# Up to six SwiGLU pairs instead of seven kept for the output stage, with a fourth piece buffer, loads ahead of stores and three late gates moved back

## The chip, the cores and the metric

The kernel runs on one NeuronCore of a Trainium2 chip. TensorE (PE) multiplies, VectorE (DVE), ScalarE (ACT) and GpSimd (POOL) do the elementwise work, and transfers are issued from SyncE's queue (SP) and from POOL. The metric is the device time of one execution in microseconds, lower being better. The changed kernel is compared with the kernel before by the medians of such times.

## The reference

One decoder block for 512 tokens, all in float32. Two token mixers (a gated convolution and a gated linear recurrence) run beside each other and are merged; then comes a SwiGLU channel mixer with 2816 inner channels, and a last normalisation. The change lies in the second half:

```python
    m = jax.nn.sigmoid(z_ga) * y_a + jax.nn.sigmoid(z_gb) * y_b
    x = x + m @ w_mix_out[l]
    h = rmsnorm(x, norm2_g[l])
    x = x + (jax.nn.silu(h @ ffn_w1[l]) * (h @ ffn_w3[l])) @ ffn_w2[l]
return rmsnorm(x, norm_f_g)
```

## The kernel before

Every float32 product is made of three products of rounded halves (high by high, high by low, low by high), which is why most tiles come as an `h` and an `l`. A weight chunk is loaded into a `raw` buffer, ACT casts it to the high half (L123), and DVE or POOL subtracts it to get the low half (L119). The function `weights` keeps four chunks ahead of the one that PE needs.

The stages follow each other on PE: the input projection (tile `z`), the two mixers' outputs (`yb`, `ya`), their mix (`mxr`), the SwiGLU products (`fr`, and `f1`/`f3` for the first pair) and the output product (`or`).

**SwiGLU.** The 22 tiles of 128 inner channels are worked on as 11 pairs, k = 0 to 10. All but the first are computed by Strassen's scheme in Winograd's form, with seven products of quarter blocks in place of eight: class `Seven`. `half()` makes the first product into the PSUM bank r1 and the second into r2; `copy()` (L1461) then has ACT copy r1 to a tile `c11`, because r1 is written again later. `first()` adds r2 to it on DVE, and `out_of` (L1442) turns the sum into one quarter of the result: SiLU on ACT (L1443), then a multiplication on DVE (L1444). `rest()` makes the other products: r3, r1 again (copied to `q` by ACT at L1489), r5, r7, and r1 a third time, and ends three more quarters, the last of them from a tile `c21`. A pair's results are two tiles, `ou{k}` and `ov{k}`. Its turn takes some 21 us.

**Output product.** It is done by the same scheme. Each pair of `ou` and `ov` is first made into operands by `Sevenfold.pair`: a split of `ou` into halves (`ous{k}h` by ACT, `ous{k}l` by DVE), a sum `os` that is split too (`os1p`), and three differences (`oe` twice, `ov` once). `o7.release(keep)` does so for the pairs that wait until only `keep` are left. In `rest()` it is called in the middle of each pair with `KEPT`, a table by k; what is left over is released in the output stage, one pair for each step. After its eleven steps the operands `oe` and `ov` are split in turn (`oeb`, `ovb`).

**Sums of weights.** The scheme needs sums and differences of weight quarters, which are computed on the chip. For `ffn_w1` and `ffn_w3` pieces (`fws`) are loaded during the earlier stages by the generator `make_f_sums`, summed on POOL and stored to DRAM (`fs`). For `ffn_w2`, 21 pieces (`fwso`, 512 KB) and two last ones of `fws` are loaded by POOL's queue during SwiGLU, summed on DVE and stored to DRAM (`ot`, `fs`). Function `out_step` moves these along, twice for each pair. A piece lives in a buffer of the pool `wsums`, of which there are `PIECES`; at the start of the kernel the same buffers hold the input x.

Tiles of 128x512 float32 come from a pool `long` of `SLOTS` buffers and a pool `short` of 5. The order of the work in the SwiGLU and output stages is made by a scheduler from the order in which the code is written, the buffers that are free and `tc.issue_after`, which sets an instruction behind another; each engine then runs its own list in order.

Of the kernel before, what the change touches and what calls it, by code (L numbers as in the profile page):

```python
# [8 lines left out]
F32 = mybir.dt.float32  # L9
# [4 lines left out]
P = 128  # L14
T = 512
# [10 lines left out]
NT = T // P  # L26
# [2 lines left out]
NF = DF // P  # L29


SLOTS, SHORT = 63, 5
RAW = 4
HL = 5
AHEAD = 4
SUMS_BEHIND = 3
# [8 lines left out]

PIECES = 3


OUT_PIECES = {0: "1", 1: "111", 2: "01", 3: "11", 4: "111", 5: "101", 6: "111", 7: "111", 8: "101", 9: "101", 10: "100"}
SEVEN = (1, 2, 3, 4, 5, 6, 7, 8, 9, 10)


BEGUN, BEGUN_LATER = (1, 2), (3,)
# [5 lines left out]
F_LATE, F_AT, OUT_MIX, MIX_LATE_LAG, LATE_LAG = 2, 6, 1, 2, 8  # L61
OUT_IN = 0

KEPT = {2: 1, 3: 2, 4: 3, 5: 4, 6: 5, 7: 6, 8: 7, 9: 7, 10: 7}


ROWS = [
# [18 lines left out]
def tile_block(ctx, tc, a, out):  # L86
# [4 lines left out]
    hls = pool("hls", HL)  # L91
    wsums = pool("wsums", PIECES)
    psum = pool("psum", 6, space=bass.MemoryType.PSUM)
    psum2 = pool("psum2", 2, space=bass.MemoryType.PSUM)

    def tiles(tag, bufs):
        p_ = pool(tag, bufs)
        return lambda name, dtype=F32: p_.tile([P, T], dtype, tag=tag, name=name)

    longt, shortt = tiles("long", SLOTS), tiles("short", SHORT)  # L100
# [5 lines left out]
    def bank(name):  # L106
        return psum.tile([P, T], F32, tag="mm", name=name)

    def bank2(name):
        return psum2.tile([P, T], F32, tag="cv", name=name)  # L110

    vec, act, pe, pool_e = nc.vector, nc.scalar, nc.tensor, nc.gpsimd


    newest = {}
# [5 lines left out]
    def split_to(h, l, full, eng, copy=act.copy):  # L121

        copy(h, full)  # L123
        if eng is None:
            put_off.append((l, full, h.bitcast(F32)))
            return h, l
        last = sub(eng, l, full, h.bitcast(F32))
        newest["sub" if eng is pool_e else "low"] = last.ins
        return h, l
# [16 lines left out]
    def split(name, full, eng, p_=None, copy=act.copy):  # L146
        p_ = p_ or pairt(name)
        return split_to(*p_, full, eng, copy)
# [243 lines left out]
    def piece_load(name, halves, queue=nc.sync):  # L392
        raw = wsums.tile([P, 1024], F32, tag="wsum", name=f"fws{name}")
        n = 1024 // len(halves)
        for h, src in enumerate(halves):
            queue.dma_start(raw[:, h * n : h * n + n].rearrange("p (e n) -> p e n", n=256), src)
        return raw
# [12 lines left out]
    def piece_store(raw, dest, queue=nc.sync):  # L410
        if len(dest.shape) == 4:
            dest = dest.rearrange("p m k n -> p (m k) n")
        return queue.dma_start(dest, raw.rearrange("p (m n) -> p m n", n=256))  # L413

    def make_f_sums():
# [8 lines left out]
        while todo or sums_due or stores_due:  # L424
# [3 lines left out]
            if sums_due and n >= sums_due[0][0]:  # L428
                sums_due.pop(0)[1]()
            if todo and n >= next_at and len(sums_due) + len(stores_due) + (n < stored[0] + STORED_LAG) < PIECES:  # L430
                next_at += SUMS_STEP - (n >= SUMS_DENSE) - (SUMS_EACH[0] <= n < SUMS_EACH[1])
# [80 lines left out]
        queue.dma_start(rowt[b][r : r + m, :P], src)  # L512

    x_nat = a["x"].rearrange("b (t p) d -> p (b t) d", p=P)
    wide = [wsums.tile([P, 1024], F32, tag="wsum", name=f"x{t}") for t in range(PIECES)]
    xt = [[w[:, :T], w[:, T:]] for w in wide] + [[longt(f"x{t}{h}") for h in range(2)] for t in range(PIECES, NT)]

    def load_x(t):
        if t < PIECES:
            nc.sync.dma_start(wide[t], x_nat[:, t, :])  # L520
            return
        for h in range(2):
            nc.sync.dma_start(xt[t][h], x_nat[:, t, h * T : (h + 1) * T])
# [5 lines left out]
    first = [i for i, (lo, _, _) in enumerate(parts) if lo < n_first]  # L529
# [14 lines left out]

    load_x(0)
    load_x(1)

    def rows_turned(c0, c1):
# [15 lines left out]
    def mm3(ps, ws, xs, lo_last=False):  # L564


        n = 3 * len(ws)
        i = 0
        three = [((wh, xh), (wh, xl), (wl, xh)) for (wh, wl), (xh, xl) in zip(ws, xs)]
        if lo_last:  # L570
            three = [q[:2] for q in three] + [q[2:] for q in three]
        for l, r in (q for qs in three for q in qs):
            pe.matmul(ps, l, r, start=i == 0, stop=i == n - 1)  # L573
            i += 1

    def w_tiles(key, kt, ahead=AHEAD):
        h, l = weights(key, ahead)
        return [(h[:, k, :], l[:, k, :]) for k in range(kt)]
# [86 lines left out]
    def first_sums(t):  # L665
        return root(t, half_sum(t))
# [40 lines left out]
    with tc.manual_schedule(engines={ET.PE, ET.Activation, ET.DVE, ET.SP, ET.Pool}):  # L707
# [4 lines left out]
        r1 = first_sums(1)  # L712
# [432 lines left out]
    LO, HI = HALVES  # L1145
# [213 lines left out]
    out_stores, out_n, sums_due = [], [0], []  # L1359
    out_at, out_steps = [None, None], {k: list(v) for k, v in OUT_PIECES.items()}  # L1360

    def due_sums(now=False):
        for entry in list(sums_due):
            entry[0] -= 1
            if now or entry[0] <= 0:
                sums_due.remove(entry)
                with tc.issue_after(newest["now"]), tc.issue_after(newest["low"]):
                    piece_sums(*entry[1], vec)

    def out_step(k):  # L1370
        due_sums(True)
        if out_at[1]:
            with tc.issue_after(newest["full"]):
                out_stores.append(piece_store(*out_at[1], pool_e).ins)
        if out_at[0]:
            sums_due.append([SUMS_BEHIND, out_at[0]])
        out_at[1], out_at[0] = out_at[0], None
        steps = out_steps.get(k)
        if steps and int(steps.pop(0)):
            name, halves, dest = out_todo.pop(0)  # L1380


            with tc.issue_after(([newest["full"]] * 2 + out_stores)[out_n[0]]):
                out_at[0] = piece_load(name, halves, pool_e), dest
            out_n[0] += 1

    def ffn_out(j, p1, p3):
        s_ = shortt(f"si{j}")
        act.activation(s_, p1, AF.Silu)

        def make(cs, dst):
            newest["now"] = vec.tensor_tensor(out=dst, in0=s_[:, cs], in1=p3[:, cs], op=ALU.mult).ins

        o7.tile(j, make)
# [22 lines left out]
    def f_product(k, got, ps, x_, w_, again=False, ahead=AHEAD, between=None):  # L1417
# [3 lines left out]
        for i in range(2):  # L1421
# [17 lines left out]
                emit_to(emitted[0] + 1)  # L1439
            due_sums()  # L1440

    def out_of(c, dst):  # L1442
        act.activation(c[:, LO], c[:, LO], AF.Silu)  # L1443
        newest["now"] = vec.tensor_tensor(out=dst, in0=c[:, LO], in1=c[:, HI], op=ALU.mult).ins  # L1444

    class Seven:
# [13 lines left out]

        def copy(self):  # L1461
            self.c11 = shortt(f"c11_{self.k}")
            act.copy(self.c11, self.r1)

        def first(self):
            add(self.c11, self.r2, self.c11)
            out_of(self.c11, self.uv[0][:, LO])

        def fourth(self, c):

# [12 lines left out]
        def rest(self):  # L1483
            k, got, r1, (u_, v_) = self.k, self.got, self.r1, self.uv
            r3, r5, r7 = bank(f"fr3_{k}"), bank2(f"fr5_{k}"), bank(f"fr7_{k}")
            f_product(k, got, r3, "s4", "b22")
            f_product(k, got, r1, "s2", "t2", True)
            q = shortt(f"q_{k}")
            act.copy(q, r1)  # L1489
            f_product(k, got, r5, "s1", "t1")  # L1490
            add(q, r5, q)
            c12 = shortt(f"c12_{k}")
            add(c12, r3, q)
            out_of(c12, u_[:, HI])
            out_step(k)

            o7.release(KEPT.get(k, 0))
            f_product(k, got, r7, "s3", "t3")
            c21 = self.c21
            if c21 is None:  # L1500
                c21 = shortt(f"c21_{k}")
                act.copy(c21, r7)
            else:
                add(c21, r1, c21)
                add(c21, r7, c21)
            add(q, r7, q)
            out_of(q, v_[:, HI])
            if self.c21 is None:
                f_product(k, got, r1, "a22", "t4", True)
                add(c21, r1, c21)  # L1510
            out_of(c21, v_[:, LO])
            out_step(k)
            o7.uv.append((u_, v_))
            o7.waiting.append((k, u_, v_))
# [36 lines left out]
    for k in range(KF):  # L1551
        if k in SEVEN:
            b = begun.pop(k, None)
            if not b:
                b = Seven(k)
                b.half()
                b.first()
                out_step(k)
            b.rest()
            continue  # L1560
        o7.release(KEPT.get(k, 0))
        o7.kept = KEPT.get(k, 0)
        for j in (2 * k, 2 * k + 1):
            p1, p3 = bank(f"f1_{j}"), bank(f"f3_{j}")
            mm3(p1, w_tiles(f"f1_{j}", ND), h2)
            mm3(p3, w_tiles(f"f3_{j}", ND), h2)
            ffn_out(j, p1, p3)
        out_step(k)
        if k + 1 in SEVEN:
            for j in BEGUN_LATER:  # L1570
                b = begun[j] = Seven(j)
                b.half()
                b.first()
                out_step(k + 1)
                for c in range(4):
                    b.fourth(c)
                b.fourth_end()
# [128 lines left out]
```

## Time and profile before

| | us |
|---|---|
| median of 3 runs | 790.12 |
| lowest and highest of them | 788.48, 792.69 |
| profiled execution, its own time | 787.58 |
| span of its instructions | 785.8 |
| PE busy | 778.2 (99%) |
| DVE busy | 679.3 (86%) |
| ACT busy | 473.5 (60%) |
| POOL busy | 362.9 (46%) |

The span reaches from the first instruction of the program to the last; the rest of the execution's own time lies around it. In the rows of a timeline the first number is the start in microseconds from the start of the span, the second the time taken, and what stands in brackets is the idle time of the engine just before, with what ended it. A busy PE may hold pauses, since the ends of matmuls are modelled; so the starts of successive matmuls are looked at too. "PEld" is the loading of weights into PE.

### The profile page before, as it was taken

Reading aid. Unit: us, or ns where it says so; the run is one execution under the profiler, and the core shown is the slowest. Engines: PE = TensorE matmul, PEld = TensorE weight load, DVE = VectorE, ACT = ScalarE, POOL = GpSimd, SP = SyncE. Lnnn points to the kernel's source line nnn. Section 1 sums busy time; section 2 is a strip of 40 time slices with the busy share of each in tenths; the row PEclk is TensorE's granted clock in tenths of the full one; section 3 lists DMA queues with packets and bytes.
Section 4 is the critical chain, followed back from the end, with each engine's and each line's share of the span. In section 5 each row is a group of like instructions: output and inputs, shape, how many; then the busy total and the mean of one; then the engine's idle time right before and its main releaser. Section 6 shows DMA issues by size and latency. Waiting matters only on the chain.

```text
span 785.8 us, 12508 instructions
## 1 busy us (share of the span) xinstructions
PE 778.2 (99%) x4328; PEld 680.6 (87%) x4328; DVE 679.3 (86%) x1074; ACT 473.5 (60%) x696; POOL 362.9 (46%) x353
## 2 busy tenths in 40 slices
PE   9999999999999999999999999999999999999996
PEld 8988888888888888888888898999999999888885
DVE  6389998889987987999799869897887889999956
ACT  7543678966785786574245676445445555556844
POOL 4367876789788989754530380122323322000000
PEclk9999999999999999999999999999999999999999
DMA  7657989899999868998978575699999999878652
GB/s 225 189 144 211 267 225 269 230 277 272 260 266 280 266 195 251 309 299 285 314 252 297 172 216 181 193 306 307 308 335 331 314 315 318 268 235 278 194 172 108
DMA packets 188561, 199.04 MB, mean 253 GB/s; under 512 B 15290, under 2 KB 149586, under 8 KB 188498
## 3 DMA queue, kind: packets, MB, share of 16 engines
q1 hardware_dynamic: 178066, 161.80, 67.4%
q0 software_dynamic: 10272, 36.18, 13.9%
q8 instruction: 34, 0.56, 0.3%
q14 instruction: 29, 0.24, 0.1%
q10 hardware_dynamic: 160, 0.27, 0.1%
HBM read 146.30 MB, written 38.80 MB: 236 GB/s over the span
## 4 chain that ended last, share of the span: by engine, by line
PE 99%; DVE 0%; ACT 0%; issue 0%
PE z L573 36%; PE fr L1432 25%; PE or L1195 13%; PE yb L573 7%; PE ya L573 6%; PE mxr L1195 5%; PE f L573 3%; PE g L1021 2%; PE fr L1477 1%; PE warm L543 1%; PE tx L635 0%; PE th L618 0%; PE z L689 0%; ACT of L1647 0%; PE orl L1195 0%; PE par_ps L552 0%
## 5 line engine op out<-in xcount | busy, mean ns | idle before, releaser
L821 DVE SCALAR_TENSOR_TENSOR cv<-u,par,cv 128x507 f32<-128x507 f32 (+15 forms) x240 | 162.2, 733 | 4.2 <-ACT cv L817 3.3
L119 POOL TENSOR_TENSOR hl_in<-raw_in,hl_in 128x1024 fp32r<-128x1024 f32 (+1 forms) x52 | 123.3, 2382 | 54.5 <-ACT hl_in L123 40.7
L119 POOL TENSOR_TENSOR fws<-fws 128x256 f32<-128x256 f32 x114 | 92.4, 812 | 38.9 <-DMA fws<-in_ffn_w_dram 33.4
L413 POOL DMA_DIRECT2D ot<-fwso x21 | 15.4, 732 | 140.9 <-DVE fwso L119 140.9
L1432 PE MATMUL fr<-hs_0h,hl_ft 128*128 128x256 f32 x320 | 59.2, 283 | 0.0
L119 DVE TENSOR_TENSOR hl_ft<-raw_ft,hl_ft 128x1024 fp32r<-128x1024 f32 x39 | 47.6, 1219 | 6.1 <-ACT hl_ft L123 6.0
L123 ACT CAST hl_in<-raw_in 128x1024 fp32r<-128x1024 f32 x50 | 51.4, 1047 | 1.3 <-PE z L573 1.1
L1432 PEld LDWEIGHTS fr<-hs_0h,hl_ft 128*128 128x128 f32 x320 | 50.6, 192 | 0.0
L123 ACT CAST hl_ft<-raw_ft 128x1024 fp32r<-128x1024 f32 x40 | 41.2, 1044 | 10.8 <-PE fr L1432 7.9
L1432 PE MATMUL fr<-hs_0l,hl_ft 128*128 128x256 f32 x160 | 45.3, 283 | 0.0
L123 ACT CAST hl_fb<-raw_fb 128x1024 fp32r<-128x1024 f32 x30 | 31.4, 1048 | 20.1 <-DMA raw_fb<-in_ffn_w_dram 9.3
L573 PE MATMUL z<-h10h,hl_in 128*128 128x512 f32 (+1 forms) x108 | 41.1, 382 | 0.0
L573 PE MATMUL z<-h13h,hl_in 128*128 128x512 f32 (+1 forms) x108 | 40.8, 379 | 0.0
L573 PE MATMUL z<-h14h,hl_in 128*128 128x512 f32 (+1 forms) x108 | 40.8, 379 | 0.0
L573 PE MATMUL z<-h15h,hl_in 128*128 128x512 f32 (+1 forms) x108 | 40.8, 379 | 0.0
L573 PE MATMUL z<-h16h,hl_in 128*128 128x512 f32 (+1 forms) x108 | 40.8, 379 | 0.0
L573 PE MATMUL z<-h12h,hl_in 128*128 128x512 f32 (+1 forms) x108 | 40.8, 379 | 0.0
L573 PE MATMUL z<-h11h,hl_in 128*128 128x512 f32 (+1 forms) x108 | 40.8, 379 | 0.0
L573 PE MATMUL z<-h17h,hl_in 128*128 128x512 f32 (+1 forms) x108 | 40.8, 379 | 0.0
L119 POOL TENSOR_TENSOR hl_ot<-raw_ot,hl_ot 128x1024 fp32r<-128x1024 f32 x1 | 2.4, 2405 | 82.8 <-ACT hl_ot L123 82.8
L123 ACT CAST hl_ob<-raw_ob 128x1024 fp32r<-128x1024 f32 (+1 forms) x23 | 23.4, 1016 | 23.8 <-PE or L1195 12.6
L119 DVE TENSOR_TENSOR hl_fb<-raw_fb,hl_fb 128x1024 fp32r<-128x1024 f32 x29 | 35.3, 1221 | 2.4 <-ACT hl_fb L123 2.4
(948 smaller groups left out, 2635.7 us busy)
## 6 DMA issues: line engine op xcount, KB each, us to landing
raw_in<-in_w_in_dram SPq DMA_DIRECT2D x51, 512.0 KB
fws<-in_ffn_w_dram SPq DMA_DIRECT2D x38, 512.0 KB
raw_ft<-fs SPq DMA_DIRECT2D x34, 512.0 KB
fs<-fws POOLq DMA_DIRECT2D x25, 512.0 KB, 5.7
fwso<-in_ffn_w_dram POOLq DMA_DIRECT2D x42, 256.0 KB, 7.1
ot<-fwso POOLq DMA_DIRECT2D x21, 512.0 KB, 5.3
raw_ob<-in_ffn_w_dram SPq DMA_DIRECT2D x33, 256.0 KB
raw_ot<-ot SPq DMA_DIRECT2D x33, 256.0 KB
```

What stands on the lines that cost most here:

```text
L119: return eng.tensor_tensor(out=o, in0=x, in1=y, op=ALU.subtract)
L123: copy(h, full)
L413: return queue.dma_start(dest, raw.rearrange("p (m n) -> p m n", n=256))
L543: pe.matmul(wp[:, :P], ones, ones, start=True, stop=True)
L573: pe.matmul(ps, l, r, start=i == 0, stop=i == n - 1)
L821: vec.scalar_tensor_tensor(out=acc[:, s:], in0=u[c][:, : T - s], scalar=dw(c, s), in1=acc[:, s:], op0=ALU.mult, op1=ALU.add)
L1021: pe.matmul(ps[:HB], head_chunk[0][:ROWS_G, g, h % 2, m, :], ext[h][m][:ROWS_G], start=m == 0, stop=m == 1)
L1195: pe.matmul(banks[i][:, cs], l_[:, ts], r_[:, cs], start=start and n == 0, stop=stop and n == 2, skip_group_check=again)
L1432: pe.matmul(ps[:, HALVES[i]], lw[:, c, :], rx_, start=not (again or i or c or m), stop=bool(i and c == 3 and m == 2), skip_group_check=True,)
L1477: pe.matmul(self.r4[:, HALVES[i]], lw, rx_, start=not (i or c or m), stop=bool(i and c == 3 and m == 2), skip_group_check=True)
```

## The change

- `KEPT` is 6, not 7, for k = 8, 9 and 10. Pairs 1, 2 and 3 are made into operands one pair earlier, and seven pairs, not eight, are left for the output stage.
- `SLOTS` goes from 63 to 61, `PIECES` from 3 to 4: two buffers of 2 KB a partition are given up, and one of 4 KB is added. At the start x still lies in three of the wide buffers.
- `out_step` issues the load of the next piece ahead of the store of the last one, and the first three loads, not two, wait for no store. The load with number n then waits for store n-3, not n-2.
- `left_over`: the gate (`out_of`) of `c21`, the last quarter of a pair, is written behind ACT's copy of the next pair's r1 (`copy()`); the gate of `c11` is written behind ACT's copy to `q`. The copies read PSUM banks that PE will write again.

```diff
-SLOTS, SHORT = 63, 5
+SLOTS, SHORT = 61, 5
-PIECES = 3
+PIECES = 4
-KEPT = {2: 1, 3: 2, 4: 3, 5: 4, 6: 5, 7: 6, 8: 7, 9: 7, 10: 7}
+KEPT = {2: 1, 3: 2, 4: 3, 5: 4, 6: 5, 7: 6, 8: 6, 9: 6, 10: 6}
...
     def out_step(k):
         due_sums(True)
-        if out_at[1]:
-            with tc.issue_after(newest["full"]):
-                out_stores.append(piece_store(*out_at[1], pool_e).ins)
-        if out_at[0]:
-            sums_due.append([SUMS_BEHIND, out_at[0]])
-        out_at[1], out_at[0] = out_at[0], None
+        stored, begun_ = out_at[1], out_at[0]
+        if begun_:
+            sums_due.append([SUMS_BEHIND, begun_])
+        out_at[1], out_at[0] = begun_, None
         steps = out_steps.get(k)
         if steps and int(steps.pop(0)):
             name, halves, dest = out_todo.pop(0)
-            with tc.issue_after(([newest["full"]] * 2 + out_stores)[out_n[0]]):
+            with tc.issue_after(([newest["full"]] * 3 + out_stores)[out_n[0]]):
                 out_at[0] = piece_load(name, halves, pool_e), dest
             out_n[0] += 1
+        if stored:
+            with tc.issue_after(newest["full"]):
+                out_stores.append(piece_store(*stored, pool_e).ins)
...
+    left = []
+
+    def left_over(behind):
+        while left:
+            with tc.issue_after(behind):
+                out_of(*left.pop(0))
...
         def copy(self):
             self.c11 = shortt(f"c11_{self.k}")
-            act.copy(self.c11, self.r1)
+            left_over(act.copy(self.c11, self.r1).ins)
-        def first(self):
+        def first(self, wait=False):
             add(self.c11, self.r2, self.c11)
-            out_of(self.c11, self.uv[0][:, LO])
+            if wait:
+                left.append((self.c11, self.uv[0][:, LO]))
+            else:
+                out_of(self.c11, self.uv[0][:, LO])
...
             q = shortt(f"q_{k}")
-            act.copy(q, r1)
+            left_over(act.copy(q, r1).ins)
...
-            out_of(c21, v_[:, LO])
+            if k + 1 in SEVEN and k + 1 not in BEGUN + BEGUN_LATER:
+                left.append((c21, v_[:, LO]))
+            else:
+                out_of(c21, v_[:, LO])
             out_step(k)
```

PE's list of instructions is the same in both kernels. Three places show what moves on the others. In their rows the line is that of the kernel in question, and the last number of a name tells apart buffers of one name.

**ACT where pair 8 ends and pair 9 begins.** `c_8` is pair 8's `c21`, `c_9` pair 9's `c11`, `fr` a PSUM bank, and the casts make weight chunks or operands. Before:

```order
L123 CAST hl_ft_9_6848<-raw_ft_9_6846 128x1024
L1443 ACTIVATE c_8_6797<-c_8_6797 128x256
L1463 COPY c_9_6875<-fr_9_6844 128x512
L123 CAST hl_ft_9_6879<-raw_ft_9_6877 128x1024
L1443 ACTIVATE c_9_6875<-c_9_6875 128x256
L123 CAST ous1h<-ou_4576 128x512
L123 CAST hl_ft_9_6929<-raw_ft_9_6927 128x1024
L123 CAST hl_fb_10_6947<-raw_fb_10_6944 128x1024
L1489 COPY q_6978<-fr_9_6844 128x512
```

Now:

```order
L123 CAST hl_ft_9_6859<-raw_ft_9_6857 128x1024
L1470 COPY c_9_6886<-fr_9_6855 128x512
L1450 ACTIVATE c_8_6810<-c_8_6810 128x256
L123 CAST hl_ft_9_6892<-raw_ft_9_6890 128x1024
L123 CAST hl_ft_9_6940<-raw_ft_9_6938 128x1024
L123 CAST hl_fb_10_6958<-raw_fb_10_6955 128x1024
L1499 COPY q_6989<-fr_9_6855 128x512
L1450 ACTIVATE c_9_6886<-c_9_6886 128x256
L123 CAST ous2h<-ou_4578 128x512
```

Both copies from the bank now stand ahead of the SiLU that stood ahead of them, two casts of weights stand ahead of the second SiLU, and the operand cast in this place is pair 2's, not pair 1's.

**DVE in the second half of pair 8.** Before:

```order
L1144 TENSOR_TENSOR c_8_6763<-fr_8_6665,q_6731 128x512
L1144 TENSOR_TENSOR q_6731<-fr_8_6667,q_6731 128x512
L1444 TENSOR_TENSOR ou_6590<-c_8_6763 128x256
L1444 TENSOR_TENSOR ov_6591<-q_6731 128x256
L119 TENSOR_TENSOR hl_ft_9_6816<-raw_ft_9_6814,hl_ft_9_6816 128x1024
```

Now:

```order
L1145 TENSOR_TENSOR c_8_6763<-fr_8_6663,q_6729 128x512
L1145 TENSOR_TENSOR os_6772<-ov_4577 128x256
L1145 TENSOR_TENSOR q_6729<-fr_8_6665,q_6729 128x512
L1451 TENSOR_TENSOR ou_6588<-c_8_6763 128x256
L119 TENSOR_TENSOR os1p_6774<-os_6772,os1p_6774 128x256
L119 TENSOR_TENSOR oe_6777<-ou_4576,ov_4577 128x256
L119 TENSOR_TENSOR hl_ft_9_6829<-raw_ft_9_6827,hl_ft_9_6829 128x1024
L119 TENSOR_TENSOR ov_4577<-os_6772,ou_4576 128x256
L1451 TENSOR_TENSOR ov_6589<-q_6729 128x256
L119 TENSOR_TENSOR oe_6777<-ou_4576,ov_4577 128x256
```

Pair 1's sum, split and differences now stand among pair 8's own additions and gates, around the low half of a weight chunk.

**POOL in the same part of SwiGLU.** Before:

```order
L396 DMA fwso_0_6407<-in_ffn_w_dram 128x2x256 x2
L413 DMA ot_101<-fwso_1_6332 512x1x256
L396 DMA fwso_1_6513<-in_ffn_w_dram 128x2x256 x2
L413 DMA ot_102<-fwso_0_6407 512x1x256
L396 DMA fwso_0_6587<-in_ffn_w_dram 128x2x256 x2
```

Now:

```order
L396 DMA fwso_0_6404<-in_ffn_w_dram 128x2x256 x2
L413 DMA ot_101<-fwso_0_6257 512x1x256
L396 DMA fwso_1_6512<-in_ffn_w_dram 128x2x256 x2
L413 DMA ot_101<-fwso_1_6329 512x1x256
L396 DMA fwso_0_6584<-in_ffn_w_dram 128x2x256 x2
```

Loads and stores still take turns, but the store behind a load is now that of the piece two loads back (`6257` behind `6404`), where it was that of the piece just before (`6332` behind `6407`).

More of the change, by code (lines that the diff above doesn't have):

```diff
@@ L514, in tile_block @@
     x_nat = a["x"].rearrange("b (t p) d -> p (b t) d", p=P)
-    wide = [wsums.tile([P, 1024], F32, tag="wsum", name=f"x{t}") for t in range(PIECES)]
-    xt = [[w[:, :T], w[:, T:]] for w in wide] + [[longt(f"x{t}{h}") for h in range(2)] for t in range(PIECES, NT)]
+    WIDE = 3
+    wide = [wsums.tile([P, 1024], F32, tag="wsum", name=f"x{t}") for t in range(WIDE)]
+    xt = [[w[:, :T], w[:, T:]] for w in wide] + [[longt(f"x{t}{h}") for h in range(2)] for t in range(WIDE, NT)]
     def load_x(t):
-        if t < PIECES:
+        if t < WIDE:
             nc.sync.dma_start(wide[t], x_nat[:, t, :])
@@ L1556, in tile_block @@
                 b.half()
-                b.first()
+                b.first(True)
                 out_step(k)
```

## The prediction

> **What bounds the kernel now.** I read the page's busy times first, then PE's waits, then busy time by stretches, then the timeline of PE. The page, the two rows that are all of PE's waits, and three stretches (us, then busy time and instructions of PE, PEld, DVE, ACT, POOL, then granted clock, DMA share, GB/s):
>
> ```profile
> span 785.8 us, 12508 instructions
> PE 778.2 (99%) x4328; PEld 680.6 (87%) x4328; DVE 679.3 (86%) x1074; ACT 473.5 (60%) x696; POOL 362.9 (46%) x353
> ...
> PE warm L543 <- DVE ones L536: 1.1, 1, 1.1
> PE tx L635 <- issue: 0.4, 1, 0.4
> ...
> 600.00:640.00 40.00, 40.00 (x335) 40.00 (x335) 31.11 (x51) 18.46 (x25) 12.55 (x18) 1.00 0.97 321
> 680.00:720.00 40.00, 40.00 (x178) 33.14 (x177) 39.75 (x72) 23.84 (x36) 0.72 (x1) 1.00 0.79 253
> 780.00:786.00 6.00, 0.00 (x0) 0.00 (x0) 1.91 (x7) 1.19 (x4) 0.49 (x1) 0.85 0.47 175
> ```
>
> PE waited 1.1 and 0.4 us at the very start and nowhere else. A full PE could still hide pauses, so I looked at the starts of matmuls:
>
> ```profile
> 641.81 0.40 PE L1432 MATMUL fr<-hs_1h,hl_fb 128*128 128x256 f32 x2
> 642.05 0.28 PE L1432 MATMUL fr<-hs_1l,hl_fb 128*128 128x256 f32 x1
> 642.17 0.40 PE L1432 MATMUL fr<-hs_1h,hl_fb 128*128 128x256 f32 x2
> ...
> 779.46 0.28 PE L1195 MATMUL or<-hl_ot,ovb10l 128*128 128x256 f32 x1
> ```
>
> Three matmuls begin in 642.17 - 641.81 = 0.36 us, 0.12 us each, and 40 us of SwiGLU hold 335, which is 40 / 335 = 0.119 us. So the beat has no pauses in it. PE ends at 779.46 + 0.28 = 779.74; the last 6 us are the normalisation and the store, which the diff leaves alone. The order of PE's instructions is the same in both kernels. The profiled execution therefore has 1.1 + 0.4 us of PE idle that the change doesn't touch, and no stall for it to take away. Its own time is 787.58, of which 785.8 is span and 1.8 lies around it. The median of the runs is 790.12, which is 790.12 - 787.58 = 2.5 us more. Whatever these runs lose, it is not in the profile; what the profile can show is where PE's margins are thin, that is, how late something may be before PE stands still.
>
> **The gates moved behind the copies.** ACT and PE where pair 8 ends and pair 9 begins:
>
> ```profile
> 637.08 1.98 ACT L123 CAST hl_ft<-raw_ft 128x1024 fp32r<-128x1024 f32 x2
> 640.34 0.42 ACT L1443 ACTIVATE c<-c 128x256 f32<-128x256 f32 x1 [1.28 <-DVE c L1144]
> 640.66 0.57 ACT L1463 COPY c<-fr 128x512 f32<-128x512 f32 x1
> ...
> 643.01 0.28 PE L1432 MATMUL fr<-hs_0h,hl_ft 128*128 128x256 f32 x1
> ```
>
> The matmul at 643.01 is the first that writes r1 again, so the copy out of r1 must have ended; it ended at 640.66 + 0.57 = 641.23, and the margin is 1.78 us. Yet r1 had been ready since about 643.01 - 48 x 0.12 = 637.25, as two products of 24 matmuls lie between. The copy was late because the SiLU ahead of it on ACT stood 1.28 us for DVE. With the copy first, it can begin when the casts end (637.08 + 1.98 = 639.06); pair 1's operand cast, which now comes here too, takes 0.40 (below). The copy then ends at about 639.06 + 0.40 + 0.57 = 640.0, and the margin is some 3.0 us: **1.2 us wider, worth nothing while nothing is late**. The same stands at `c11`:
>
> ```profile
> 644.54 0.42 ACT L1443 ACTIVATE c<-c 128x256 f32<-128x256 f32 x1 [2.37 <-DVE c L1144]
> 644.87 0.60 ACT L123 CAST ous1h<-ou 128x512 fp32r<-128x512 f32 x1
> 645.38 1.04 ACT L123 CAST hl_ft<-raw_ft 128x1024 fp32r<-128x1024 f32 x1
> ...
> 646.45 1.22 DVE L119 TENSOR_TENSOR hl_ft<-raw_ft,hl_ft 128x1024 fp32r<-128x1024 f32 x1 [0.25 <-ACT hl_ft L123]
> ...
> 650.45 0.40 PE L1432 MATMUL fr<-hs_1h,hl_ft 128*128 128x256 f32 x2
> ...
> ACT c L1443 <- DVE c L1144: 40.0, 20, 3.7
> ```
>
> That SiLU held ACT for 2.37 us with a weight cast behind it; DVE waited 0.25 for the cast, and PE needed DVE's result (646.45 + 1.22 = 647.67) at 650.45, a margin of 2.78. In the new order two weight casts come ahead of this SiLU. In all ACT stood 40 us for `c` in 20 places between 500 and 690; the idle time is not the path, the thin margins behind it are. What is late instead is the gate itself, by a few us; its result goes to `ou` or `ov`, which no one reads until the pair is released, six or seven pairs later or, for the last pairs, in the output stage. That cover is tens of us, so the price is nothing. From below the row bounds the gain at 0 in this execution, from above at the 2.5 us that the median lies over it.
>
> **One pair out of the output stage.** A pair's work on DVE and ACT (ns: least, median, most):
>
> ```profile
> 645.50 0.69 DVE L119 TENSOR_TENSOR ous1l<-ou,ous1h 128x512 fp32r<-128x512 f32 x1
> 653.91 0.42 DVE L1144 TENSOR_TENSOR os<-ov 128x256 f32<-128x256 f32 x1
> ...
> L119 DVE TENSOR_TENSOR os1p<-os,os1p x11: 409/414/421, 494.9 to 710.5; 128x256 fp32r<-128x256 f32 x11
> ...
> L119 DVE TENSOR_TENSOR oe<-ou,ov x22: 408/414/425, 495.2 to 711.8; 128x256 f32<-128x256 f32 x22
> ...
> L123 ACT CAST os1p<-os x11: 397/402/408, 493.3 to 708.6; 128x256 fp32r<-128x256 f32 x11
> ```
>
> On DVE: 0.69 + 0.42 (`os`) + 0.41 (`os1p`) + 2 x 0.41 (`oe`) + 0.41 (`ov`, the same shape) = 2.75 us; on ACT: 0.60 + 0.40 = 1.0 us. So pairs 8, 9 and 10 each keep one pair's work (pair 8 gets it anew, at 31.11 of 40 us busy DVE), and the output stage loses one. There DVE is busy 39.75 us of 40 between 680 and 720, the tightest place of the second half. Its margin:
>
> ```profile
> 694.99 1.21 DVE L119 TENSOR_TENSOR hl_ob<-raw_ob,hl_ob 128x1024 fp32r<-128x1024 f32 x1
> ...
> 699.20 0.62 PE L1195 MATMUL or<-hl_ob,ous6h 128*128 128x512 f32 x2
> ```
>
> The chunk is ready at 696.20 and first read by the second matmul of this row, at about 699.4: 3.2 us. Take 2.75 us off DVE ahead of it and it is up to 5.9. Again nothing is won where nothing stalls; the bounds are 0 and the same 2.5 us.
>
> **Loads ahead of stores, four piece buffers.**
>
> ```profile
> 643.08 0.74 POOL L413 DMA_DIRECT2D ot<-fwso  x1 [8.26 <-DVE fwso L119]
> 643.73 1.41 POOL L396 DMA_DIRECT2D fwso<-in_ffn_w_dram  x2
> ...
> POOL fwso L396 <- DMA ot<-fwso: 5.5, 3, 2.7
> ...
> DVE fwso L119 <- DMA fwso<-in_ffn_w_dram: 10.8, 4, 3.6
> ```
>
> Here a load stood behind a store that had waited 8.26 us for DVE's sums. Now it goes first, so it can start up to 8.26 us earlier (at the least the store's own 0.74), and the three waits for a buffer's store (5.5 us) should vanish. DVE, which runs in order, stood four times between 500 and 690 (10.8 us) for a piece that had not landed, with weight subtractions queued behind; earlier loads shorten that. The store goes 1.41 us later at the most behind its load, and the chunks that read it back are wanted only in the output stage, tens of us on. The bytes are the same. In the earlier stages the fourth buffer moves a few loads of `fws` by some places in SP's queue; PE has no wait there, so I take nothing.
>
> **The sum.** Profiled: 787.6 + 0 + 0 + 0 = 787.6. The runs' excess of 2.5 us should shrink, not go: margins elsewhere are thinner and untouched, such as in the mix, where `x` is read out of a bank that PE needs next:
>
> ```profile
> 442.68 0.68 DVE L1144 TENSOR_TENSOR x<-mxr,x 128x512 f32<-128x512 f32 x1
> ...
> 443.72 0.39 PE L1195 MATMUL mxr<-mxt40h,mxvb0h 128*128 128x512 f32 x1
> ```
>
> The margin is 443.72 - 443.36 = 0.36 us. I take two thirds to three quarters of the excess as gained, which leaves 0.7: **788.3 us**, or 0.2% less than 790.12. A measurement of this kernel can't tell less than about 0.5% (4 us) from no change, so this counts as none.
>
> **Rivals.**
>
> *Faster than that* (chance 0.12). If all the excess sits in the margins widened here, the time is 787.6, still only 0.3% less than 790.12. For over 0.5% the kernel before must be nearer to its slowest run, 792.69, in the comparison: (792.69 - 787.6) / 792.69 = 0.6%. For it speak the spread of the runs and the 40 us of waits at `c`; against it, that PE's beat is a floor which the change does not lower.
>
> *Slower: earlier pieces get in front of the weights* (0.08). In 600 to 640 transfers take 0.97 of the engines' time and move 321 GB/s; a piece of 512 KB is 0.524 MB / 321 GB/s = 1.6 us of it. ACT already waits for weights there:
>
> ```profile
> ACT hl_fb L123 <- DMA raw_fb<-in_ffn_w_dram: 7.6, 5, 1.9
> ```
>
> If two pieces, 3.3 us, run ahead of a chunk with the 2.78 us margin of above, PE stalls 0.5 us; with two pieces for each of seven pairs that is 14 x 0.5 = 7 us, and 787.6 + 7 = 795. It decides from 2.78 us of delay on. Against it: each load replaces one that came later, nothing is added, and the same order of ACT widens that margin. The Trainium skill, page "DMA: Bandwidth & Descriptors", section "Issuing engines are not separate DMA queues", says that transfers started by any engine end up on the same 16 DMA engines and interleave there. By that rule POOL's loads are in no lane of their own, which is what this rival needs; the share of 0.97 agrees with it.
>
> *Slower: too few buffers* (0.04). A pair made into operands holds five `long` buffers (two for `ous`, one each for `os1p`, `oe`, `ov`) instead of two, so 3 more are held from pair 8 on, of 2 fewer. If the cast `ous1h` must wait for a buffer until the next pair, weight casts wait behind it on ACT. A pair's turn is the distance of these copies:
>
> ```profile
> 619.16 0.57 ACT L1463 COPY c<-fr 128x512 f32<-128x512 f32 x1
> ```
>
> 640.66 - 619.16 = 21.5 us; less the margin of 2.78 that is 18.7, and the time 806. Against it: in the new lists pair 1's operands stand exactly one pair earlier, so the scheduler found buffers for them there. The same rows answer the rival that the change doesn't do what it says.
>
> **How the numbers follow.** No measurable change 0.76; faster 0.12; slower 0.08 + 0.04 = 0.12. The range goes from 786.4 (the floor of 787.6 less 1.2 us, half of the excess, by which the runs compared may differ from the profiled one) to 792.2 (about the slowest run before, should the excess stay and scatter). The two slower cases lie outside, as does a part of the faster one.
>
> **What would show it.** In the changed profile PE again has no wait but the 1.1 and 0.4 us, and the span is within 1 us of 785.8. Each `COPY c<-fr` comes ahead of its SiLU and ends about 3 us before r1 is written again. ACT's 40 us for `c` fall by a third or more. POOL's waits for `ot` stores are gone and DVE's 10.8 us for `fwso` are nearly so; DVE in 680 to 720 is below 39.75 or runs further ahead of PE. The prediction is wrong if PE waits in a new place, with ACT or DVE there standing for a piece or a buffer, or if the median falls below 786.

## The result, and the profile after

| | before | changed |
|---|---|---|
| median, us | 789.65 | 787.80 |
| lowest to highest (22 runs each), us | 787.54 to 792.69 | 787.49 to 788.83 |
| runs above 789 us | 14 of 22 | none |
| profiled execution, its own time, us | 787.58 | 787.77 |

The ratio of the changed kernel to the one before is 0.9979, with a 95% interval of 0.9970 to 0.9987: 0.21% less, which counts as no change by the bound of 0.5%, though the interval leaves 1 out. The fastest runs of the two kernels are the same within 0.05 us. What the change did is to take away the upper part of the spread.

The page of the changed kernel and all of PE's waits:

```profile
span 786.0 us, 12507 instructions
...
PE 777.9 (99%) x4328; PEld 680.4 (87%) x4328; DVE 683.6 (87%) x1074; ACT 474.5 (60%) x696; POOL 363.4 (46%) x353
...
PE warm L544 <- DVE ones L537: 1.1, 1, 1.1
PE tx L636 <- issue: 1.0, 1, 1.0
```

PE waits nowhere but at the start, as before. The span is 0.2 us longer; PE's matmuls, compared one by one, are 0.22 us behind those of before from 30 us on, and no further behind at the end. So the two profiled executions, both near the floor, can't show the gain; they show what became of the other engines. ACT's longest waits between 500 and 690 us:

```profile
ACT hl_ft L123 <- PE fr L1432: 18.5, 13, 2.5
ACT q L1499 <- PE fr L1432: 18.0, 10, 1.8
ACT c L1512 <- PE fr L1432: 12.3, 7, 2.1
ACT c L1470 <- PE fr L1432: 11.0, 7, 1.8
ACT c L1450 <- DVE c L1145: 1.5, 2, 1.3
ACT hl_fb L123 <- DMA raw_fb<-in_ffn_w_dram: 1.1, 1, 1.1
```

The 40.0 us for which the SiLU stood for DVE's `c` are 1.5 now. The copies out of PSUM (L1470, `q` L1499) wait for PE instead: ACT is ready for them before their data are, which is the right way round for an engine that is not to hold PE up. The wait for weights (`raw_fb`) fell from 7.6 to 1.1 us. The same place as before, the end of pair 8, in the timeline:

```profile
637.73 0.59 ACT L1470 COPY c<-fr 128x512 f32<-128x512 f32 x1 [1.84 <-PE fr L1432]
638.21 0.42 ACT L1450 ACTIVATE c<-c 128x256 f32<-128x256 f32 x1
...
643.23 0.28 PE L1432 MATMUL fr<-hs_0h,hl_ft 128*128 128x256 f32 x1
```

The copy ends at 637.73 + 0.59 = 638.32 and r1 is written again at 643.23: the margin is 4.9 us, where it was 1.78. Now POOL's waits between 460 and 700 us:

```profile
POOL ot L413 <- DVE fwso L119: 122.7, 17, 31.2
POOL fwso L396 <- DMA ot<-fwso: 23.3, 8, 3.9
```

and DVE's between 500 and 690:

```profile
DVE hl_ft L119 <- ACT hl_ft L123: 9.6, 16, 1.7
DVE hl_fb L119 <- ACT hl_fb L123: 8.3, 14, 1.3
```

Among DVE's waits there is no `fwso` any more: it never stood for a piece. POOL's loads, on the other hand, stand longer for stores than before. One piece, followed through both kernels, shows why that costs nothing. Before, POOL:

```profile
621.58 0.73 POOL L413 DMA_DIRECT2D ot<-fwso  x1 [8.26 <-DVE fwso L119]
622.23 0.71 POOL L396 DMA_DIRECT2D fwso<-in_ffn_w_dram  x1
```

and DVE's first sum of that piece:

```profile
630.65 0.88 DVE L119 TENSOR_TENSOR fwso<-fwso 128x256 f32<-128x256 f32 x2 [3.51 <-DMA fwso<-in_ffn_w_dram]
```

The load could not start until a store ahead of it had waited 8.26 us for DVE's sums of the piece before; then DVE stood 3.51 us for the load, with the weight subtractions behind it (two of `hl_fb` came right after). DVE held POOL up and POOL then held DVE up. From issue to first use were 630.65 - 622.23 = 8.4 us. The load issued at about that time in the changed kernel, POOL and then DVE:

```profile
621.13 1.41 POOL L396 DMA_DIRECT2D fwso<-in_ffn_w_dram  x2
623.10 0.73 POOL L413 DMA_DIRECT2D ot<-fwso  x1 [0.56 <-DVE fwso L119]
```

```profile
636.63 0.42 DVE L119 TENSOR_TENSOR fwso<-fwso 128x256 f32<-128x256 f32 x1
```

636.63 - 621.13 = 15.5 us, and no wait. Counted from the first, that load is already the next piece, the 19th; the 18th, which the rows of before show, is this one:

```profile
611.67 1.41 POOL L396 DMA_DIRECT2D fwso<-in_ffn_w_dram  x2 [3.46 <-DMA ot<-fwso]
```

Its load goes out 622.23 - 611.67 = 10.6 us earlier than before, and DVE begins its sums at 625.54, 13.9 us after that and 5.1 us earlier than before. Over the pieces from the fifth on, the time from issue to first use is 7.4 to 16.0 us before and 12.8 to 28.5 now.

### The profile page after: what moved, and what is told of

The parts are those of the page before. It is cut to its first block, busy times and chain, and to the rows that moved or that the text cites. A ratio compares the mean times of both kernels' runs of the same rounds, so it can differ in the third digit from the quotient of the medians.

```text
span 786.0 us, 12507 instructions
## 1 busy us (share of the span) xinstructions
PE 777.9 (99%) x4328; PEld 680.4 (87%) x4328; DVE 683.6 (87%) x1074; ACT 474.5 (60%) x696; POOL 363.4 (46%) x353
## 4 chain that ended last, share of the span: by engine, by line
PE 99%; DVE 0%; issue 0%; ACT 0%
PE z L574 36%; PE fr L1432 25%; PE or L1196 13%; PE yb L574 7%; PE ya L574 6%; PE mxr L1196 5%; PE f L574 3%; PE g L1022 2%; PE fr L1487 1%; PE warm L544 1%; PE tx L636 0%; PE th L619 0%; PE z L690 0%; ACT of L1660 0%; PE orl L1196 0%
## 5 line engine op out<-in xcount | busy, mean ns | idle before, releaser
L396 POOL DMA_DIRECT2D fwso<-in_ffn_w_dram x42 | 29.8, 714 | 26.4 <-DMA ot<-fwso 23.3
```

## The experiments

The kernel before was run beside each group. "Above 789" counts runs that lasted longer than 789 us. The intervals are those of the ratio to the kernel before of the same group (medians 789.87, 789.82 and 789.64 in 28, 35 and 33 runs).

| kernel | median | range | above 789 | ratio, interval |
|---|---|---|---|---|
| gates_only | 791.34 | 788.02 to 794.38 | 9 of 12 | 1.0013 [0.9998, 1.0029] |
| pieces_only | 787.90 | 787.55 to 788.98 | 0 of 9 | 0.9979 [0.9969, 0.9988] |
| kept_only | 789.98 | 788.02 to 792.61 | 10 of 12 | 1.0004 [0.9992, 1.0015] |
| no_gates | 787.61 | 787.46 to 787.68 | 0 of 6 | 0.9973 [0.9962, 0.9984] |
| order_only | 788.17 | 787.48 to 791.85 | 5 of 12 | 0.9989 [0.9977, 1.0001] |
| buffers_only | 789.76 | 788.16 to 791.33 | 8 of 11 | 1.0002 [0.9990, 1.0014] |
| no_piece_wait | 788.59 | 787.56 to 790.49 | 2 of 11 | 0.9982 [0.9973, 0.9992] |
| sums_later | 789.13 | 787.82 to 790.08 | 6 of 11 | 0.9990 [0.9981, 0.9999] |
| stand_in_gates | 788.27 | 787.41 to 790.14 | 3 of 11 | 0.9987 [0.9976, 0.9998] |
| load_after | 791.80 | 789.82 to 794.50 | 12 of 12 | 1.0028 [1.0014, 1.0042] |
| load_pieces | 788.25 | 787.93 to 789.49 | 1 of 11 | 0.9982 [0.9974, 0.9991] |
| sums_earlier | 787.74 | 787.55 to 789.41 | 1 of 9 | 0.9977 [0.9968, 0.9987] |

### Which of the three edits it is

**gates_only**: the kernel before with the gates moved, and nothing else.

```diff
-            act.copy(self.c11, self.r1)
+            left_over(act.copy(self.c11, self.r1).ins)
...
-            act.copy(q, r1)
+            left_over(act.copy(q, r1).ins)
...
-                b.first()
+                b.first(True)
```

> The kernel before with the three late gates moved behind ACT's copies, and nothing else. Theory G (the runs of before lose their 2 us where ACT's copies out of r1 stand behind a SiLU that waits for DVE): the median falls from about 789.6 to about 788, with no run above 789. Theory P (they lose it where DVE stands for a piece of weights that has not landed): no change, 789 to 790, with runs up to 792. Theory K (they lose it in the output stage, where DVE is full): no change either.

It is no faster than before; the middle of its interval is slower. Its profile caught a long execution, of 791.2 us, which shows where such a run loses its time. All of PE's waits in it:

```profile
PE warm L543 <- DVE ones L536: 1.1, 1, 1.1
PE tx L635 <- issue: 1.0, 1, 1.0
PE or L1195 <- DVE c L1144: 0.8, 1, 0.8
PE or L1195 <- DVE x2b L1144: 0.5, 1, 0.5
PE fr L1432 <- DVE hl_ft L119: 0.3, 1, 0.3
```

and of DVE's waits between 500 and 690 us those for a transfer:

```profile
DVE fwso L119 <- DMA fwso<-in_ffn_w_dram: 12.1, 3, 4.1
DVE fws L119 <- DMA fws<-in_ffn_w_dram: 3.5, 1, 3.5
```

PE stands for DVE at the end of SwiGLU and in the output stage. The rows above hold 1.6 us of such waits. Compared matmul by matmul with the profile of before, its starts fall 3.6 us behind between 640 and 740 us, and 791.2 - 787.6 = 3.6 is the excess of this execution. DVE meanwhile stood 15.6 us for pieces in four places. The gates out of the way did not shorten that.

**pieces_only**: the kernel before with `SLOTS` 61, `PIECES` 4 and the new `out_step`, but with its own `KEPT` and gates.

```diff
-SLOTS, SHORT = 63, 5
+SLOTS, SHORT = 61, 5
-PIECES = 3
+PIECES = 4
...
+        if stored:
+            with tc.issue_after(newest["full"]):
+                out_stores.append(piece_store(*stored, pool_e).ins)
```

> The kernel before with four piece buffers, 61 long buffers and loads ahead of stores, and nothing else. Theory P: about 787.8 and no run above 789; DVE's waits for fwso (10.8 us in 4 places before) are gone. Theories G and K: 789 to 790, and runs up to 792.

This has the whole gain, with the same ratio as the changed kernel, and no wait of DVE for a piece. ACT still stood 19.7 us for `c`, half of the 40.0 of before; sums_earlier, below, has the gain with 38.7 us of them, so those waits were not what cost time.

**kept_only**: the kernel before with the new table.

```diff
-KEPT = {2: 1, 3: 2, 4: 3, 5: 4, 6: 5, 7: 6, 8: 7, 9: 7, 10: 7}
+KEPT = {2: 1, 3: 2, 4: 3, 5: 4, 6: 5, 7: 6, 8: 6, 9: 6, 10: 6}
```

> The kernel before with at most six pairs kept, and nothing else. Theory K: about 788, no run above 789. Theories G and P: 789 to 790, with runs up to 792.

Nothing: the interval lies around 1, and the upper part of the spread is there. Its profiled execution lasted 790.07 us; PE's waits in it:

```profile
PE or L1195 <- DVE x2b L1144: 1.2, 2, 1.0
PE tx L635 <- issue: 1.1, 1, 1.1
PE warm L543 <- DVE ones L536: 1.1, 1, 1.1
```

Again PE stands for DVE in the output stage, though one pair's work was taken out of it. So the place that theory K names is one where long executions lose time; that one pair fewer there would help is what the run speaks against.

**no_gates**: the changed kernel with the gates where they were before.

```diff
-            left_over(act.copy(self.c11, self.r1).ins)
+            act.copy(self.c11, self.r1)
...
-            left_over(act.copy(q, r1).ins)
+            act.copy(q, r1)
```

> The changed kernel without the move of the gates. Theory P: still about 787.8. Theory G: back to 789 or more. Theory K: about 788.

787.61 in six runs that lie within 0.22 us: as good as the changed kernel, whose median is 787.80, or better. Of the three edits only that of the pieces matters.

### What it is about the pieces

**order_only**: the new `out_step`, with three buffers and 63 slots.

```diff
-        if out_at[1]:
-            with tc.issue_after(newest["full"]):
-                out_stores.append(piece_store(*out_at[1], pool_e).ins)
...
-            with tc.issue_after(([newest["full"]] * 2 + out_stores)[out_n[0]]):
+            with tc.issue_after(([newest["full"]] * 3 + out_stores)[out_n[0]]):
...
+        if stored:
+            with tc.issue_after(newest["full"]):
+                out_stores.append(piece_store(*stored, pool_e).ins)
```

**buffers_only**: `PIECES` 4 and `SLOTS` 61, with the old `out_step`.

```diff
-SLOTS, SHORT = 63, 5
+SLOTS, SHORT = 61, 5
-PIECES = 3
+PIECES = 4
```

> The kernel before with the load of a piece ahead of the store, in the three buffers it had. Theory O (the order does it, because a load no longer waits for DVE's sums of the piece just before): DVE's waits for fwso fall from 10.8 us to under 4, the median to 788 to 788.5. Theory B (the fourth buffer does it): no change, 789.5 to 790.

> The kernel before with four piece buffers and 61 long ones, but stores still ahead of loads. Theory O: no change, 789.5 to 790, DVE's waits for fwso still about 10 us. Theory B: 787.8, and the waits gone.

The fourth buffer alone does nothing; in the old order the load stands behind the store on POOL whichever buffer it is to fill. The order alone splits its runs: 7 of 12 lie at the floor, at 788.19 or below, and 5 from 789.38 up. Its waits on POOL between 460 and 700 us:

```profile
POOL fwso L396 <- DMA ot<-fwso: 77.2, 15, 8.2
POOL ot L413 <- DVE fwso L119: 58.2, 8, 31.1
```

With three buffers the load that now stands ahead of the store still waits for a store to land, 77.2 us in 15 places against 23.3 in 8 with four, and DVE still stood for pieces, 7.0 us in four places against 10.8, where theory O expected under 4. The interval of order_only includes 1 and that of pieces_only doesn't: the order by itself probably brings part of the gain, and order and buffer together bring it in every run.

**no_piece_wait**: the kernel before (`SLOTS` 61 to make room), DVE's sums read a tile of zeros in place of the piece.

```diff
-                    piece_sums(*entry[1], vec)
+                    piece_sums(stand_in, entry[1][1], vec)
```

> The kernel before, but DVE's sums of the pieces loaded during SwiGLU are made on a stand-in tile of zeros (61 long buffers make room for it): the same DVE instructions, no wait for a piece; the pieces are stored as loaded, so the output product uses wrong sums. If DVE's standing for pieces is the cause: 787.6 to 788, no run above 789, though ACT's gates and the seven kept pairs are as before. If not: 789.5 to 790.

More changes than DVE's wait: the stores no longer wait for DVE's sums either (140.9 us of POOL's waits before, none now), so all pieces are loaded sooner. The median falls by 1.2 us to 788.59, about two thirds of the 1.85 that the change brings, but the runs do not all come to the floor. The profiled one was the longest of its eleven, at 790.49, and its longest wait of PE is a new one:

```profile
PE fr L1434 <- ACT c L1465: 1.6, 1, 1.6
```

That is a copy of r1, at 604.89 us, that came too late on ACT, the margin that the gates edit widens; at 597.25 ACT had stood 4.82 us for a chunk of weights (`raw_fb`). **stand_in_gates** puts that edit on top:

```diff
                     piece_sums(stand_in, entry[1][1], vec)
...
-            act.copy(self.c11, self.r1)
+            left_over(act.copy(self.c11, self.r1).ins)
```

> The run in which DVE waits for no piece (sums on a stand-in tile, pieces stored as loaded, wrong sums in the output product), with the three gates moved behind ACT's copies as well. That run had a median of 788.59 and runs up to 790.49, and its profile one pause of 1.6 us where PE waited for a copy out of r1 on ACT. If the place of the gates matters once the copies are late: 787.7 to 788, no run above 789, no wait of PE for ACT. If the pause came from late transfers that hold ACT itself: 788.3 to 788.8 again.

788.27 against 788.59, and 3 of 11 runs above 789: the place of the gates is not what remains. (The profiled execution is a short one, 787.57, so it doesn't show where the long ones lose time.) Both runs are long at times though DVE never stands for a piece, so such stands can't be the only way to a long execution. In both, ACT's waits for weights (`raw_fb` and `raw_ft`) come to some 35 us between 500 and 690, where before has 7.8 and the change 1.7; but sums_earlier, below, has 18.8 and runs near the floor. Whether the rest is due to them was not tried.

**sums_later** and **sums_earlier** change one number in the kernel before: how many steps after a piece its sums are written, if the next `out_step` doesn't come first.

```diff
-SUMS_BEHIND = 3
+SUMS_BEHIND = 9
```

```diff
-SUMS_BEHIND = 3
+SUMS_BEHIND = 1
```

> The kernel before with the sums of a piece started nine half products behind the step, not three. If sums, store and next load form a loop in which each waits for the one before, the loads come later, DVE stands longer for them, and the median rises to 791 to 794. If the pieces don't matter: 789.5 to 790.

> The kernel before with the sums of a piece started one half product behind the step, not three. Its opposite, nine half products, was expected to be slower and came out at 789.13. If DVE's wait is set by a load that follows the sums of the piece before, earlier sums let the load start as much earlier and the median stays at 789.5 to 790. If what counts is how far the loads run ahead of PE: 788 to 788.8. If what counts is the time between a piece's load and its sums: above 790.

Later sums were to lengthen the loop of store, load and sums; they did not, the median is 0.7 us below that of before. In that form the theory of the loop falls: a later sum gives the load more time to land as well as holding the store back. Earlier sums have the whole gain, 0.9977, with three buffers, the old `out_step`, the old gates and the old table; their 787.74 is below all three values that were expected. DVE still stood for pieces, and this is the row between 500 and 690 us:

```profile
DVE fwso L119 <- DMA fwso<-in_ffn_w_dram: 7.4, 5, 2.0
```

Five waits, none above 2.0 us, where before four reached 3.6 (and the one for `fws` is 2.9 us, not 4.5). The piece followed above, in POOL's list of this kernel:

```profile
619.34 0.73 POOL L413 DMA_DIRECT2D ot<-fwso  x1 [6.99 <-DVE fwso L119]
619.99 0.71 POOL L396 DMA_DIRECT2D fwso<-in_ffn_w_dram  x1
```

Its load was issued 622.23 - 619.99 = 2.2 us earlier against a PE that runs at the same beat, and DVE began its sums at 628.59, not 630.65. So it is not the sum of DVE's waits that decides; what fits is how late DVE comes out of them. Stands up to 2.9 us are in the profiles of kernels that mostly run near the floor (this one and order_only); stands of 3.6 to 4.8 us are in the profiles of short executions (787.58, before; 788.16, buffers_only) and of long ones (789.99, sums_later; 790.07, kept_only; 791.2, gates_only). Against the margins that the prediction read, 1.78 to 3.2 us, the first are about covered, the second only if nothing else is late. That is an argument from these rows; the stand was not set by itself to a given length.

The long profiles also show where the time goes. With the matmuls counted by number, PE's starts fall behind those of the profile of before as follows (us):

| profile | its own time | up to 600 | 600 to 640 | 640 to 720 | 720 to 740 | after |
|---|---|---|---|---|---|---|
| gates_only | 791.20 | 0.0 | 0.0 | 2.4 | 1.2 | 0.0 |
| kept_only | 790.07 | 0.2 | 0.0 | 0.6 | 1.8 | 0.0 |
| sums_later | 789.99 | 0.2 | 0.9 | 0.0 | 1.3 | 0.0 |
| no_piece_wait | 790.49 | 1.1 | 1.8 | 0.0 | 0.0 | 0.0 |

In the three that keep DVE's waits for pieces, 1.2 to 1.8 us are lost between 720 and 740, where PE goes over to `oeb` and `ovb` and DVE's additions (`x2b`) must empty its banks. In these three DVE also leaves SwiGLU late: its last gate (`ov<-c`) begins at 683.1 to 685.3 us, and at 679.5 to 682.3 in the profiles of executions below 789. In 680 to 720 DVE is busy 39.7 to 40.0 us of 40 there, so what it is late by, it can hardly make up. This fits a delay that begins at the pieces in SwiGLU and is paid, for a good part, tens of us later in the output stage; no run sets such a delay by itself.

### Whether the other two edits give room

DVE was loaded with six more operations of 128x384 for each of seven pairs, on a tile that is no longer read, in the changed kernel (**load_after**) and in pieces_only (**load_pieces**).

```diff
-                add(c21, r1, c21)
+                with tc.issue_after(add(c21, r1, c21).ins):
+                    for _ in range(6):
+                        vec.tensor_tensor(out=par[:, :384], in0=par[:, :384], in1=par[:, :384], op=ALU.max)
```

> The changed kernel with six DVE instructions (128x384, about 0.55 us each) added at the end of each of ten pairs, on a tile that nobody reads any more: 33 us of DVE work in SwiGLU. If the moved gates and the sixth instead of the seventh kept pair give room when DVE is late, this one is at least 1.5 us faster than the same load on the pieces alone. If they give none, the two are within 1 us.

> The kernel before with four piece buffers and loads ahead of stores alone, and the same six DVE instructions for each pair. If gates and kept pairs give room: 1.5 us or more slower than the changed kernel with the same load, with PE waiting for ACT's copies out of r1 or in the output stage. If they give none: within 1 us of it.

The line stands in a branch that three of the ten pairs don't take: the profiles have 42 such operations, not 60, and DVE's busy time grows by 699.1 - 683.6 = 15.5 us, not by 33. The outcome is the reverse of what was expected. With the load, the pieces alone stay near the floor, while the whole change becomes 791.80, that is 791.80 - 788.25 = 3.5 us longer. PE's waits in load_after:

```profile
PE or L1196 <- DVE x2b L1145: 2.6, 2, 1.9
```

and ACT and then DVE ahead of the longer one, at PE's 723.51 us:

```profile
719.95 1.05 ACT L123 CAST hl_ot<-raw_ot 128x1024 fp32r<-128x1024 f32 x1 [2.65 <-DMA raw_ot<-ot]
```

```profile
721.03 1.23 DVE L119 TENSOR_TENSOR hl_ot<-raw_ot,hl_ot 128x1024 fp32r<-128x1024 f32 x1 [2.04 <-ACT hl_ot L123]
722.17 0.68 DVE L119 TENSOR_TENSOR ovb1l<-ov,ovb1h 128x512 fp32r<-128x512 f32 x1
722.77 0.68 DVE L1145 TENSOR_TENSOR x2b<-or,x2b 128x512 f32<-128x512 f32 x1
```

A chunk of sums read back from DRAM (`raw_ot`) came late, ACT stood 2.65 us for it, DVE 2.04 for ACT, and the addition that empties PE's bank, behind it on DVE, came 1.9 us too late. In load_pieces ACT waited 0.6 us for such chunks and PE not at all. The loads of `raw_ot` were issued late: SP's queue came to the first at 711.22 us, in load_pieces at 707.94. The two kernels also differ in more than the gates and the table: in them alone, of all these kernels, PE's own list changed too, each with another order of some products, most of them between 722 and 728 us, right behind the first stall. Whether that order, `KEPT` or the gates bring the stall about was not tried apart, so this pair of runs doesn't tell what the two edits are worth. In 680 to 720 us DVE was busy 38.11 of 40 in load_after and 40.00 in load_pieces, so it is not a lack of DVE's time in the output stage.

## Why the prediction was right, and where it wasn't

**The floor and the excess: right.** The floor of 787.6 held: in all kernels but load_after, the fastest run lies between 787.41 and 788.16, whatever was edited. The gain is in the runs' excess over it. Against the floor, before has 789.65 - 787.6 = 2.05 us and the change 0.2, so nine tenths were gained where the prediction took two thirds to three quarters. That step was mis-sized by 0.5 us. No row gave that share, and the forecast started from a median of three runs that lay 0.5 us above the one of 22: that the gain in us came out as forecast (1.85 against 790.12 - 788.3 = 1.8) is partly luck.

**The gates moved: right in the trace, worth nothing in time.** The wait for `c` fell by far more than a third, and the margin at the copy is 4.9 us, more than the 3.0 that was worked out, as ACT has done its casts earlier and no operand cast stands ahead of the copy. But gates_only and no_gates show that the excess does not hang on it. The step that fails is "from above at the 2.5 us that the median lies over it": the prediction counted this margin among those whose widening brings the gain, gave it the first place, and did not say which of the three edits carries how much.

**One pair out of the output stage: wrong in its margin, and worth nothing.** "Take 2.75 us off DVE ahead of it and it is up to 5.9". The rows in the changed kernel, DVE and then PE:

```profile
694.82 1.22 DVE L119 TENSOR_TENSOR hl_ob<-raw_ob,hl_ob 128x1024 fp32r<-128x1024 f32 x1
695.95 0.42 DVE L119 TENSOR_TENSOR ov<-os,ou 128x256 f32<-128x256 f32 x1
696.29 0.68 DVE L119 TENSOR_TENSOR ous8l<-ou,ous8h 128x512 fp32r<-128x512 f32 x1
```

```profile
699.42 0.61 PE L1196 MATMUL or<-hl_ob,ous6h 128*128 128x512 f32 x2
```

The chunk is ready at 696.04 and read at about 699.64: 3.6 us, and in pieces_only, without this edit, 3.6 as well. The step that fails is "off DVE ahead of it": the output stage releases one pair at each step, so the same operations stand ahead of this chunk as before, those of one pair further on (`ous8l` behind it, where pieces_only has `ous7l` at 696.84). What the edit takes away falls at the end of the row of pairs: `ous10l` is made at 703.9 us instead of 708.4. "DVE in 680 to 720 is below 39.75" came true with 38.50:

```profile
680.00:720.00 40.00, 40.00 (x178) 33.15 (x177) 38.50 (x68) 24.29 (x36) 0.71 (x1) 1.00 0.82 261
```

**Loads ahead of stores: right in what it does to DVE, wrong on POOL.** DVE's 10.8 us for pieces are gone, and pieces_only has the whole gain. That it comes through these waits is argued, not shown, since sums_earlier has it too with 7.4 us of them left. And "the three waits for a buffer's store (5.5 us) should vanish" failed; they are 23.3 us in eight places. A load that no longer waits for DVE's sums comes to wait for the store before to land. No cost of it shows, as the loads are nevertheless issued earlier than before: 10.6 us for the piece followed above.

**The rivals.** Earlier pieces in front of the weights: ACT's wait for `raw_fb` went from 7.6 to 1.1 us, the opposite of what that rival needs. The Trainium skill, page "DMA: Bandwidth & Descriptors", section "Issuing engines are not separate DMA queues", has all engines' transfers share the same 16 DMA engines. no_piece_wait, whose last piece is loaded at 588 us instead of 662, has 34.9 us of waits of ACT for weights, which fits that; a loss of time from it is not shown. Too few buffers: PE never waits for an operand, and the median is far from 806. Faster by over 0.5% would have needed, over this floor, a median of before of 787.6 / 0.995 = 791.6 or more, and it was 789.65.

## What to carry to other kernels

Where a profile shows the bounding engine without a wait and the median lies above the profiled time, look for the pair of in-order engines that hold each other up: here a load behind a store behind DVE's sums, and DVE's next work behind the load. Issue the load of the next piece ahead of the store of the last, with one buffer more, so that the load goes out earlier; or, for the price of one number, write the sums sooner. Judge such an edit by the spread of many runs, and each part by itself: the two parts here that changed the trace most visibly, ACT's waits and DVE's load, gained no time.

## What was not expected of the hardware

With the same lists of instructions, executions of the kernel before differ by 5 us, while PE's beat between its pauses is the same in all profiles. The landings of the pieces don't tell a long execution from a short one. From issue to landing, the loads of pieces (L396) between 500 and 700 us took, in the kernel before (787.58 us):

```profile
DMA to landing us min/median/max: 5.4/7.3/8.9
```

in the changed kernel (787.77 us):

```profile
DMA to landing us min/median/max: 5.1/7.2/8.8
```

and in gates_only (791.20 us):

```profile
DMA to landing us min/median/max: 5.5/7.5/9.3
```

Landings that vary by 3.5 to 3.8 us in one execution are as large as the margins of DVE's chunks, so a kernel with thin margins may stall on them; but they vary as much in the short executions as in the long one, and what makes one execution long and the next short stays open. What the experiments show is that the spread goes, in all runs or all but one, in three kernels that issue the loads earlier (pieces_only, no_gates and sums_earlier), and that in order_only and no_piece_wait it goes only in part.
